# Other byte offsets for the weight blocks of the 256-column products in a two-layer encoder kernel

## The chip, the cores and the metric

The kernel runs on one core of a Trainium2 chip, in one launch. The metric is the device time of that launch in microseconds. Before the change three timed runs gave a median of 1366.84 us (1366.77 to 1368.76).

## What is computed

The reference is a trunk of two encoder layers on 512 tokens of width 1024, in float32. Each layer has a token mixer and a channel mixer, each between two RMS norms, with a residual sum:

```
hn = rms_norm(x, norm_mix_pre)
m  = retention_na_mixer(hn, ...)        # layer 0: retention beside 2-D neighbourhood attention
m  = ssd_mixer(hn, ...)                 # layer 1: bidirectional Mamba-2 mixer
x  = x + rms_norm(m, norm_mix_post)
u  = depthwise_conv_centered(rms_norm(x, norm_ffn_pre) @ w_up, conv_w, conv_b)   # 1024 -> 2 x 2816
gate, val = split(u, 2)
f  = (gelu(gate) * val) @ w_down        # 2816 -> 1024
x  = x + rms_norm(f, norm_ffn_post)
```

Most of the time is matrix products with weights from DRAM: the input projections of the mixers, and `w_up` and `w_down` of the channel mixers.

## The kernel before, in words

**Products in three terms.** TensorE takes float32 operands here in a one-pass format (float32r). To keep the precision, each operand is split into a high part and a low part: ScalarE casts the source to the high part and VectorE subtracts it from the source for the low part (`split`, lines 115 and 116). A product is then three matmuls that add up in one PSUM bank (`mm3`, lines 124 to 126): high weights with high data (L124), low weights with high data (L125), high weights with low data (L126). Each matmul first loads 128 x 128 weights into the array (LDWEIGHTS, the engine PEld of the profile), then streams 512 or 256 columns of data. One 128 x 128 block of weights is 128 float32 wide, 512 bytes in each partition.

**The ring.** A weight unit of 128 x 1024 float32 lands from DRAM in a staging tile `wst` and is split into a place of `ring`. The ring has four places, taken in turn (`weight`, line 82). A place is 2,048 + 128 float32 wide, 8,704 bytes or 17 x 512, and the ring begins on a multiple of 512 bytes; so all four places lie alike within 512 bytes. The 128 spare floats (`GAP`) let the two parts be shifted:

```
SKEW, GAP = 16, 128                      # line 29
a, b = skew, 1024 + GAP - 3 * skew       # in weight(): starts of the high and the low part
```

With `skew=0` both parts begin on a 512-byte boundary (0, and 1,152 floats or 9 x 512 bytes). With `skew=SKEW` of 16 the high part begins 64 bytes behind a boundary and the low part at 1,104 floats, 4,416 bytes, which is 320 behind one. Since all eight blocks of a part follow at 512 bytes, every weight load from that part has the same offset. The data operands (`xh`, `xl` and the combinations below) begin on multiples of 512 bytes in every product.

**Where 256 columns are streamed.** Nearly all products stream 512 columns and use `skew=0`. Three places stream 256 columns and use `skew=SKEW`:

- *Strassen blocks.* Of the 22 column groups of 128 in each half of `w_up` (gate and value), four pairs (`UP`, line 396: 6, 10, 14, 18) are computed by Strassen's scheme with seven products where there would be eight (`up_strassen`, line 437). A product is 2 x 4 x 3 = 24 matmuls of 256 columns. Its weights are made by `weights(i)` (line 458), which loads, adds and splits into the ring through `parts` (line 450). Its data are `A11`, `A12`, `A22` (parts of `xh`, `xl`) or the combinations `R1`, `S3`, `S2`, `S4` (`combos`, line 399), in the fixed order of line 480. With four blocks in each of two layers that makes 8 blocks, 56 products and 1,344 matmuls.
- *The start of each feed-forward stage* (`ffn`, from line 531). Four units, two column groups of gate and value each, run first over tokens 0 to 255 and then over tokens 256 to 511, since the last two token tiles are still being normalised and transposed when the first half begins (`E.flush()`, line 546, issues those transposes between the units). Two units lie in the ring, the third in two tiles `b1h` and `b1l` (high and low apart), the fourth in one tile `s3` (both parts). `extra` (line 526) places these at `SKEW` floats behind the tile's start, so both parts have 64 bytes. 4 x 2 x 8 x 3 = 192 matmuls in each layer. In the second layer the first two units are made ahead, in `trunk` (line 1334).
- *The start of mixer 1* (line 1228). Three units in the ring, in the same two halves: 144 matmuls.

The order of the work is written out by hand in the source, with priorities for the splits. One queue (SP's) issues the weight loads, POOL's issues the DRAM-to-DRAM sums of `w_down`.

Of the kernel before, what the change touches and what calls it, by code (L numbers as in the profile page):

```python
# [25 lines left out]
HK = NF // 2  # L26
HW = S // 2
QUARTER = HK * P * S
SKEW, GAP = 16, 128


class Env:
# [49 lines left out]
    def weight(self, skew=0):  # L82

        place = self.ring[:, self.turns % 4]
        self.turns += 1
        a, b = skew, 1024 + GAP - 3 * skew
        return place[:, a:a + 1024], place[:, b:b + 1024]

    def wunit(self, src, parts=None, st=None, behind=None, low_behind=None, skew=0):
# [347 lines left out]
def up_strassen(E, w_up, f, X, G, V):  # L437

    nc, tc = E.nc, E.tc
    low, high = slice(0, HW), slice(HW, S)

    def load(pool, name, s, h):
        st = pool.tile([P, 1024], F32, name=name)
        nc.sync.dma_start(st.rearrange("p (f c) -> p f c", f=2),
                          w_up[s, f:f + 2, :, h * 512:h * 512 + 512].rearrange("f p c -> p f c"))
        return st

    def parts(st):  # L450
        hi, lo = E.weight(SKEW)
        E.split(hi, lo, st)
        return hi, lo

    add = lambda o, x, y: nc.vector.tensor_tensor(o, x, y, op=ALU.add)
    q = {}

    def weights(i):
        with tc.high_priority(60):
            if i == 0:  # L460
                q[11] = load(E.wst, "wst", 0, 0)
                return parts(q[11])
            if i == 1:
                q[12], q[22] = load(E.wst, "wst", 1, 0), load(E.wst, "wst", 1, 1)
                add(q[11], q[11], q[12])
                add(q[12], q[12], q[22])
                return parts(q[12])
            if i == 2:
                q[0] = E.gain.tile([P, D], F32, name="gain")
                add(q[0], q[11], q[22])  # L470
                return parts(q[0])
            if i == 3:
                q[21] = load(E.gain, "gain", 0, 1)
                add(q[0], q[0], q[21])
                return parts(q[0])
            return parts(q[{4: 11, 5: 21, 6: 22}[i]])

    a = [E.mm.tile([P, S], F32, name="mm") for _ in range(2)]
    b, d = ([E.px.tile([P, S], F32, name="pu", tag="px") for _ in range(2)] for _ in range(2))
    order = ("A11", a), ("S3", b), ("S2", a), ("A22", b), ("R1", a), ("A12", d), ("S4", a)  # L480
    for i, (n, bank) in enumerate(order):
        hi, lo = weights(i)
        more = i in (2, 3, 4, 6)
        for j in range(2):
            for k in range(4):
                c = slice(j * 512 + k * P, j * 512 + k * P + P)
                E.mm3(bank[j][:, :HW], hi[:, c], lo[:, c], X[n][0][:, k], X[n][1][:, k], not more and k == 0, k == 3, more)
        if i == 4:
            t = E.tmp.tile([P, 2, HW], F32, name="w5", tag="tmp")
        for j in range(2):  # L490
            r = bank[j][:, :HW]
            if i in (3, 5):
                o = G[:, j, low if i == 3 else high]
                add(o, r, o)
            else:
                o = t[:, j] if i == 4 else {0: G[:, j, high], 1: V[:, j, low], 2: G[:, j, low], 6: V[:, j, high]}[i]
                nc.scalar.copy(o, r)
        if i == 4:
            add(V[:, :, low], t, V[:, :, low])
        if i in (2, 5):  # L500
            E.chore(2)


def ffn(E, w_up, cw, w_down, ts, g_post_row, done, w1=None):


    nc, tc = E.nc, E.tc
    with ExitStack() as ctx:
        hp, cp = (ctx.enter_context(tc.tile_pool(name=n, bufs=1)) for n in ("ffn_h", "ffn_c"))
        H = hp.tile([P, NF, S], F32, name="H")  # L510

        def conv(ps, s, f, neg=False):
            w = lambda i: (cwn[:, f] if neg and i < 3 else cwt[:, s, f])[:, i:i + 1]
            o = E.tmp.tile([P, S], F32, name=f"cv{s}", tag="tmp")
            nc.scalar.activation(o, ps, AF.Identity, scale=w(1), bias=w(3))  # L515
            nc.vector.scalar_tensor_tensor(o[:, 1:], ps[:, :S - 1], w(0), o[:, 1:], op0=ALU.mult, op1=ALU.add)  # L516
            nc.vector.scalar_tensor_tensor(o[:, :S - 1], ps[:, 1:], w(2), o[:, :S - 1], op0=ALU.mult, op1=ALU.add)  # L517
            return o

        def tail(f, pg, pv, neg=False):  # L520
            g = conv(pg, 0, f)
            nc.scalar.activation(g, g, AF.Gelu_apprx_tanh)  # L522
            v = conv(pv, 1, f, neg)
            nc.vector.tensor_tensor(H[:, f], g, v, op=ALU.mult)

        def extra(tags):
            t = [hp.tile([P, SKEW + 2048 // len(tags)], R32, name="x" + n, tag=n)[:, SKEW:] for n in tags]
            t = t if len(t) == 2 else [t[0][:, :1024], t[0][:, 1024:]]
            return [x[:, c:c + 512] for x in t for c in (0, 512)]

        u0, u1, st = w1 or (E.wunit(w_up[0, 0], skew=SKEW), E.wunit(w_up[1, 0], skew=SKEW), None)

        behind = E.turned[1][1] if w1 else None
        w0 = [[u0, u1], [E.wunit(w_up[0, 1], extra(("b1h", "b1l")), st, behind=behind),
                         E.wunit(w_up[1, 1], extra(("s3",)), behind=behind)]]
        cwt = cp.tile([P, 2, NF, 4], F32, name="cwt")
        nc.sync.dma_start(cwt, cw)
        cwn = cp.tile([P, NF, 3], F32, name="cwn")
        nc.vector.tensor_scalar(cwn, cwt[:, 1, :, :3], -1.0, None, op0=ALU.mult)
        p0 = [[E.mm.tile([P, S], F32, name="mm") for s in range(2)] for f in range(2)]  # L540
        for c in range(2):
            for i in range(4):
                f, s = i // 2, i % 2
                E.proj_fm(p0[f][s], w0[f][s], c * 256, c * 256 + 256)
                if c == 0 and i in (1, 2):
                    E.flush()
        for f in range(2):
            tail(f, *p0[f])
        make = combos(E, hp, H[:, 14:].rearrange("p (n g) s -> p n (g s)", n=4).rearrange("p n (k c) -> p n k c", k=4))
        for f in range(2, NF):  # L550
            if f in UP or f - 1 in UP:
                if f in UP:
                    G, V = (cp.tile([P, 2, S], F32, name=n, tag=t) for n, t in
                            ((("G", "k0"), ("V", "k1")) if UP.index(f) % 2 else (("G", "k2"), ("V", "k3"))))
                    up_strassen(E, w_up, f, X, G, V)
                    for j in range(2):
                        tail(f + j, G[:, j], V[:, j], True)
                continue
            ps = []
            for s in range(2):  # L560
                behind = w1 and f == 2
                st = E.wload(w_up[s, f], E.mid if behind and s == 0 else None)
                w = E.wunit(None, st=st, behind=E.turned[3][1] if behind else None)
                ps.append(E.mm.tile([P, S], F32, name="mm"))
                E.proj_fm(ps[-1], w)
            tail(f, *ps)
            E.chore(2)
            if f < UP[0]:
                X = next(make)
            if f == NF - 2:  # L570
                first = [hp.tile([P, HK, HW], R32, name="a" + n, tag=n) for n in ("b1h", "b1l")]
                for k in range(0, HK, 4):
                    c = slice(k, min(k + 4, HK))
                    E.split(first[0][:, c], first[1][:, c], H[:, c, HW:])
        g_post = E.bcast(g_post_row)
        down_strassen(E, hp, cp, w_down, ts, H, first, g_post, done)
# [331 lines left out]
def mixer1(E, w_dt, w_fm, cw, dtc, cols, mask, w_out, g_post_row, done, ahead):  # L908
# [8 lines left out]
    with ExitStack() as ctx:  # L917
# [307 lines left out]
                project(o, i)  # L1225
            silus(o)

        w0 = [E.wunit(w_fm[0, i], skew=SKEW) for i in range(3)]
        p0 = [E.mm.tile([P, S], F32, name="mm") for _ in range(3)]
        for c in range(2):  # L1230
            for i, (w, ps) in enumerate(zip(w0, p0)):
# [11 lines left out]
        for g, o in enumerate(gs):  # L1243
            nx = gs[g + 1] if g + 1 < NG else None
            for step in SLOTS[g].split():
                a, i = step[0], int(step[1:] or 0)
# [22 lines left out]
        st = {}  # L1269
# [19 lines left out]
def trunk(tc, x, norms, ab, ssd, ffns, out):  # L1289

    nc = tc.nc
    with ExitStack() as ctx:
        E = Env(ctx, tc)
        w0 = []
# [35 lines left out]
        w1 = []  # L1330

        def ahead(w):
            up = ffns[1][0]
            w1.extend((E.wunit(up[0, 0], skew=SKEW), E.wunit(up[1, 0], low_behind=w, skew=SKEW), E.wload(up[0, 1])))

        mixer1(E, *ssd, norms[1, 1], then(norms[1, 2]), ahead)
        E.chores = sums(E, ffns[1][2], ts[1])
        ffn(E, *ffns[1], ts[1], norms[1, 3], store, w1)
        while E.late:
            E.flush()  # L1340
# [119 lines left out]
```

## Time and profile before

| What | Value |
|---|---|
| median of the three timed runs | 1366.84 us |
| device time of the profiled execution | 1368.77 us |
| its span, first to last instruction | 1367.0 us |
| mean granted TensorE clock | 0.999 |
| LDWEIGHTS busy | 1133.3 us |
| matmuls with `ring` weights over `xh`, `xl`, 512 columns | 840 each of L124, L125, L126, mean 392 ns |
| the same with 256 columns | 176 each, mean 281 ns |
| Strassen block in the span | 343.0 to 362.8 us (first), 1213.7 to 1233.4 us (last) |

A row of the timeline gives the start from the span's beginning, the duration, the engine, the line, and output <- inputs by the program's names with buffer numbers left out. All products of `mm3` carry the lines 124 to 126, so they are told apart by the tiles: `pu<-xh,ring` is a Strassen product with a bank of the pool `px`, `mm<-xS,ring` one with a combination S as data. `mm<-xh,xs` is the fourth unit of a feed-forward start. Durations of matmuls overlap, since one starts before the one ahead of it has drained; the rate is read from start to start.

### The profile page before, as it was taken

Reading aid. Unit: us, or ns where it says so; the run is one execution under the profiler, and the core shown is the slowest. Engines: PE = TensorE matmul, PEld = TensorE weight load, DVE = VectorE, ACT = ScalarE, POOL = GpSimd, SP = SyncE. Lnnn points to the kernel's source line nnn. Section 1 sums busy time; section 2 is a strip of 40 time slices with the busy share of each in tenths; the row PEclk is TensorE's granted clock in tenths of the full one; section 3 lists DMA queues with packets and bytes.
Section 4 is the critical chain, followed back from the end, with each engine's and each line's share of the span. In section 5 each row is a group of like instructions: output and inputs, shape, how many; then the busy total and the mean of one; then the engine's idle time right before and its main releaser. Section 6 shows DMA issues by size and latency. Waiting matters only on the chain.

```text
span 1367.0 us, 19496 instructions
## 1 busy us (share of the span) xinstructions
PE 1341.5 (98%) x7352; PEld 1133.3 (83%) x7352; DVE 1087.6 (80%) x1524; ACT 813.5 (60%) x1345; POOL 112.6 (8%) x130
## 2 busy tenths in 40 slices
PE   7999999999999999999999999999999999999997
PEld 6877777898999888888778788777878899998886
DVE  7468888697768889697878876898789887788876
ACT  5356667453554566664878787477555455556563
POOL 1011110100111100020000110000010001110000
PEclk9999999999999999999999999999999999999999
DMA  7443223126779945654566465174434678994554
GB/s 294 138 148 91 99 89 105 46 97 219 253 208 234 252 152 190 198 204 130 138 185 194 121 188 165 53 200 112 146 129 131 225 248 215 231 252 127 198 179 145
DMA packets 73471, 229.90 MB, mean 168 GB/s; under 512 B 8352, under 2 KB 9120, under 8 KB 72864
## 3 DMA queue, kind: packets, MB, share of 16 engines
q1 hardware_dynamic: 58320, 167.30, 37.5%
q0 software_dynamic: 7168, 46.14, 13.5%
q10 hardware_dynamic: 7888, 15.21, 4.2%
q8 instruction: 58, 0.95, 0.3%
q14 instruction: 37, 0.30, 0.1%
HBM read 221.01 MB, written 51.64 MB: 199 GB/s over the span
## 4 chain that ended last, share of the span: by engine, by line
PE 83%; DVE 6%; ACT 4%; DMA 3%; issue 2%; POOL 1%; SPq 0%; DVEq 0%; POOLq 0%; ACTq 0%
PE mm L124 23%; PE mm L126 23%; PE mm L125 23%; DMA pb<-pd 2%; PE pu L126 2%; PE pu L125 2%; PE pu L124 2%; PE pi L1126 1%; PE st L1075 1%; DVE ring L116 1%; PE py L1146 1%; DMA wst<-in_c_fm 1%; ACT pb L1105 1%; PE pt L181 1%; PE y L805 1%
## 5 line engine op out<-in xcount | busy, mean ns | idle before, releaser
L124 PE MATMUL mm<-xh,ring 128*128 128x512 f32 (+1 forms) x1024 | 382.0, 373 | 0.9 <-ACT z L1045 0.5
L126 PE MATMUL mm<-xl,ring 128*128 128x512 f32 (+1 forms) x1024 | 381.1, 373 | 1.0 <-DVE xl L116 0.5
L125 PE MATMUL mm<-xh,ring 128*128 128x512 f32 (+1 forms) x1024 | 380.8, 372 | 1.0 <-DVE ring L116 1.0
L116 DVE TENSOR_TENSOR ring<-wst,ring 128x1024 fp32r<-128x1024 f32 (+1 forms) x232 | 279.9, 1211 | 90.0 <-ACT ring L115 89.3
L115 ACT CAST ring<-wst 128x1024 fp32r<-128x1024 f32 (+1 forms) x232 | 239.0, 1034 | 150.1 <-PE mm L125 73.2
L124 PEld LDWEIGHTS mm<-xh,ring 128*128 128x128 f32 x1024 | 191.9, 187 | 36.3 <-issue 2.3
L126 PEld LDWEIGHTS mm<-xl,ring 128*128 128x128 f32 x1024 | 191.6, 187 | 35.5 <-issue 1.3
L125 PEld LDWEIGHTS mm<-xh,ring 128*128 128x128 f32 x1024 | 192.3, 188 | 34.3 <-DVE ring L116 1.4
L1105 ACT ACTIVATE pb<-pb,tok 128x128 f32<-128x128 f32 x256 | 80.8, 393 | 7.2 <-DMA pb<-pd 6.1
L515 ACT ACTIVATE cv<-mm,cwt 128x512 f32<-128x512 f32 x56 | 43.3, 776 | 62.9 <-PE mm L126 62.7
L124 PE MATMUL mm<-ring,ab1h 128*128 128x512 f32 x164 | 64.0, 390 | 0.0
L126 PE MATMUL mm<-ring,ab1h 128*128 128x512 f32 x164 | 63.9, 390 | 0.0
L125 PE MATMUL mm<-ring,ab1l 128*128 128x512 f32 x164 | 63.8, 389 | 0.0
L516 DVE SCALAR_TENSOR_TENSOR cv<-mm,cwt,cv 128x511 f32<-128x511 f32 x56 | 41.7, 745 | 21.2 <-ACT cv L515 21.2
L522 ACT ACTIVATE cv<-cv 128x512 f32<-128x512 f32 x44 | 27.8, 631 | 44.7 <-DVE cv L517 44.7
L1039 DVE SCALAR_TENSOR_TENSOR xf<-mm,cwt,xf 128x511 f32<-128x511 f32 (+1 forms) x64 | 47.5, 744 | 7.7 <-ACT xf L1036 7.3
L282 POOL DMA_DIRECT2D ts<-in_f_down x48 | 30.0, 658 | 259.6 <-PE mm L126 225.6
L517 DVE SCALAR_TENSOR_TENSOR cv<-mm,cwt,cv 128x511 f32<-128x511 f32 x56 | 41.7, 746 | 0.9
L1158 POOL TENSOR_TENSOR sq<-sq 128x512 f32<-128x512 f32 x11 | 16.7, 1514 | 309.2 <-ACT sq L1152 246.0
L124 PE MATMUL mm<-ring,yh 128*128 128x512 f32 x104 | 40.8, 394 | 0.7 <-DVE xf L1039 0.7
L124 PE MATMUL mm<-ring,xh 128*128 128x512 f32 x104 | 41.3, 404 | 0.0
L125 PE MATMUL mm<-ring,yl 128*128 128x512 f32 x104 | 41.1, 395 | 0.0
(359 smaller groups left out, 2918.1 us busy)
## 6 DMA issues: line engine op xcount, KB each, us to landing
wst<-in_f_up SPq DMA_DIRECT2D x80, 512.0 KB
ts<-in_f_down POOLq DMA_DIRECT2D x48, 704.0 KB, 6.1
wst<-in_c_fm SPq DMA_DIRECT2D x40, 512.0 KB
wst<-ts SPq DMA_DIRECT2D x32, 512.0 KB
pb<-pd ACTq DMA_DIRECT2D x29, 512.0 KB
wst<-in_f_down SPq DMA_DIRECT2D x24, 512.0 KB
ts<-ts POOLq DMA_DIRECT2D x16, 704.0 KB, 9.7
wst<-in_ab_fm SPq DMA_DIRECT2D x20, 512.0 KB
```

What stands on the lines that cost most here:

```text
L115: first = self.nc.scalar.copy(hi, src)
L116: second = self.nc.vector.tensor_tensor(lo, src, hi.bitcast(F32), op=ALU.subtract)
L124: mm(out, lh, rh, start=first, stop=False)
L125: mm(out, ll, rh, start=False, stop=False)
L126: self.product = mm(out, lh, rl, start=False, stop=last)
L282: out.append(lambda i=i, src=src, j=j, c=c, kw=kw: gp.dma_start(part(ts, i, c), part(src, j, c), **kw))
L515: nc.scalar.activation(o, ps, AF.Identity, scale=w(1), bias=w(3))
L516: nc.vector.scalar_tensor_tensor(o[:, 1:], ps[:, :S - 1], w(0), o[:, 1:], op0=ALU.mult, op1=ALU.add)
L517: nc.vector.scalar_tensor_tensor(o[:, :S - 1], ps[:, 1:], w(2), o[:, :S - 1], op0=ALU.mult, op1=ALU.add)
L522: nc.scalar.activation(g, g, AF.Gelu_apprx_tanh)
L1039: nc.vector.scalar_tensor_tensor(r[:, a], ps[:, b], wc(j), r[:, a], op0=ALU.mult, op1=ALU.add)
L1105: nc.scalar.activation(pb[:, dr, c], pb[:, dr, c], AF.Identity, scale=1.0 - 2 * dr, bias=tok[:, 0, c, dr * H + h:dr * H + h + 1])
```

## The change

`SKEW` becomes 48, and the low part begins at `1024 + GAP - skew // 3`. So a skewed ring place has its high part at 192 bytes within 512 and its low part at 1,136 floats, 4,544 bytes, which is 448 within 512. The distance of the two is 256 bytes within 512, as before. The tiles of `extra` have both parts at 192 bytes.

The first product of each Strassen block (`i == 0`) no longer uses the skew: its two parts begin on the boundary. The same holds for the first unit of each feed-forward start and of mixer 1's start. No instruction is added, removed or moved on any engine: the rows of all five engines are the same in the two programs, and only start addresses differ.

```diff
-SKEW, GAP = 16, 128
+SKEW, GAP = 48, 128
...
-        a, b = skew, 1024 + GAP - 3 * skew
+        a, b = skew, 1024 + GAP - skew // 3
...
-    def parts(st):
-        hi, lo = E.weight(SKEW)
+    def parts(st, i):
+        hi, lo = E.weight(SKEW if i else 0)
...
-                return parts(q[11])
+                return parts(q[11], i)
...
-        u0, u1, st = w1 or (E.wunit(w_up[0, 0], skew=SKEW), E.wunit(w_up[1, 0], skew=SKEW), None)
+        u0, u1, st = w1 or (E.wunit(w_up[0, 0]), E.wunit(w_up[1, 0], skew=SKEW), None)
...
-        w0 = [E.wunit(w_fm[0, i], skew=SKEW) for i in range(3)]
+        w0 = [E.wunit(w_fm[0, i], skew=SKEW if i else 0) for i in range(3)]
...
-            w1.extend((E.wunit(up[0, 0], skew=SKEW), E.wunit(up[1, 0], low_behind=w, skew=SKEW), E.wload(up[0, 1])))
+            w1.extend((E.wunit(up[0, 0]), E.wunit(up[1, 0], low_behind=w, skew=SKEW), E.wload(up[0, 1])))
```

More of the change, by code (lines that the diff above doesn't have):

```diff
@@ L466, in weights @@
                 add(q[12], q[12], q[22])
-                return parts(q[12])
+                return parts(q[12], i)
             if i == 2:
@@ L470, in weights @@
                 add(q[0], q[11], q[22])
-                return parts(q[0])
+                return parts(q[0], i)
             if i == 3:
@@ L474, in weights @@
                 add(q[0], q[0], q[21])
-                return parts(q[0])
-            return parts(q[{4: 11, 5: 21, 6: 22}[i]])
+                return parts(q[0], i)
+            return parts(q[{4: 11, 5: 21, 6: 22}[i]], i)
     a = [E.mm.tile([P, S], F32, name="mm") for _ in range(2)]
```

## The prediction

> **What bounds the kernel now.** I read the page first: busy time by engine, the clock in slices, the chain of waits.
>
> ```profile
> span 1367.0 us, 19496 instructions
> PE 1341.5 (98%) x7352; PEld 1133.3 (83%) x7352; DVE 1087.6 (80%) x1524; ACT 813.5 (60%) x1345; POOL 112.6 (8%) x130
> PEclk9999999999999999999999999999999999999999
> PE 83%; DVE 6%; ACT 4%; DMA 3%; issue 2%; POOL 1%; SPq 0%; DVEq 0%; POOLq 0%; ACTq 0%
> ```
>
> TensorE is busy for 98% of the span at full granted clock, and 83% of the chain that ended last is its own matmuls. Next, the waits of TensorE (total us, times, longest):
>
> ```profile
> PE pt L181 <- DVE xs L172: 9.7, 4, 7.3
> PE mm L124 <- ACT xh L115: 1.2, 2, 1.0
> ```
>
> The largest is the very start of the kernel (a norm before the first transposes), and the next is 1.2 us. So nothing is to be won from waits. A change of addresses alone can only move the time if it changes how fast matmuls follow each other, or how long VectorE and ScalarE take to write the operands. So the view that matters is the timeline of TensorE inside a Strassen block (columns: start in us, duration in us, line, operation). This is the first of the eight blocks, its first and its last rows:
>
> ```profile
> 342.77 0.39 PE L126 MATMUL mm<-xl,ring 128*128 128x512 f32 x1
> 343.00 0.28 PE L124 MATMUL mm<-xh,ring 128*128 128x256 f32 x1
> 343.12 0.28 PE L125 MATMUL mm<-xh,ring 128*128 128x256 f32 x1
> 343.24 0.28 PE L126 MATMUL mm<-xl,ring 128*128 128x256 f32 x1
> ...
> 362.67 0.28 PE L126 MATMUL mm<-xS,ring 128*128 128x256 f32 x1
> 362.79 0.40 PE L124 MATMUL mm<-xh,ring 128*128 128x512 f32 x1
> ```
>
> From 343.00 to 362.79 the block's 7 x 24 = 168 matmuls start one after another: 19.79 us / 168 = 117.8 ns from start to start, with no idle time. The durations (0.28 us) overlap and say nothing about the rate; the step between starts does. Now the start of the second feed-forward stage, where the same kind of product, from the same ring, at the same 64 and 320 bytes, runs behind a wait for VectorE:
>
> ```profile
> 1020.10 0.39 PE L126 MATMUL mm<-xl,ring 128*128 128x256 f32 x1 [0.51 <-DVE xl L116]
> 1020.32 0.28 PE L124 MATMUL mm<-xh,ring 128*128 128x256 f32 x1
> 1020.44 0.28 PE L125 MATMUL mm<-xh,ring 128*128 128x256 f32 x1
> 1020.56 0.28 PE L126 MATMUL mm<-xl,ring 128*128 128x256 f32 x1
> 1020.68 0.28 PE L124 MATMUL mm<-xh,ring 128*128 128x256 f32 x1
> 1020.79 0.28 PE L125 MATMUL mm<-xh,ring 128*128 128x256 f32 x1
> ...
> 1022.49 0.28 PE L125 MATMUL mm<-xh,ring 128*128 128x256 f32 x1
> ```
>
> From 1020.79 to 1022.49 there are 15 steps: 1.70 / 15 = 113.3 ns. So these products have two regular steps, a long one of 117.8 ns and a short one of 113.3 ns. The minimum, median and maximum of durations show how regular each is. In the Strassen blocks, and then in the stretch from 1020.4 to 1022.2:
>
> ```profile
> L124 PEld LDWEIGHTS pu<-xh,ring x128: 187/188/188, 351.4 to 1230.1; 128*128 128x128 f32 x128
> L125 PEld LDWEIGHTS pu<-xh,ring x128: 192/192/192, 351.5 to 1230.3; 128*128 128x128 f32 x128
> L125 PE MATMUL pu<-xh,ring x128: 281/281/281, 351.6 to 1230.4; 128*128 128x256 f32 x128
> ```
>
> ```profile
> L125 PE MATMUL mm<-xh,ring x6: 276/276/283, 1020.4 to 1022.2; 128*128 128x256 f32 x6
> ```
>
> In the long step every matmul takes 281 ns without exception and every third weight load 192 instead of 188; in the short step matmuls take 276. Both hold themselves: each goes on until something disturbs it. And offset alone does not choose between them. The fourth unit of each feed-forward start has both its parts at 64 bytes; it runs long in the first layer and short in the second:
>
> ```profile
> 285.44 0.28 PE L125 MATMUL mm<-xh,xs 128*128 128x256 f32 x1
> ...
> 287.91 0.28 PE L125 MATMUL mm<-xh,xs 128*128 128x256 f32 x1
> ```
>
> ```profile
> 1030.09 0.28 PE L126 MATMUL mm<-xl,xs 128*128 128x256 f32 x1
> ...
> 1030.77 0.28 PE L126 MATMUL mm<-xl,xs 128*128 128x256 f32 x1
> ```
>
> That is 2.47 / 21 = 117.6 ns, and 0.68 / 6 = 113.3 ns. What chooses is how the stretch is entered: from a stream of 512-column products (all eight Strassen blocks) it becomes the long step; behind a late operand, as at 1020.10, it passes a few uneven steps and becomes the short one.
>
> **The change, part by part.** No engine's instructions are moved, added or removed; only start addresses differ. So the sum has no term for instructions or queues.
>
> The first product of each Strassen block now lies on the boundary. The nearest rows are mixer 0's score products, also 256 columns with the weights on a 512-byte boundary, in short runs:
>
> ```profile
> 140.58 0.28 PE L789 MATMUL sc<-rql,rk 128*128 128x256 f32 x1
> ...
> 141.29 0.28 PE L789 MATMUL sc<-rql,rk 128*128 128x256 f32 x1
> ```
>
> ```profile
> 173.15 0.28 PE L789 MATMUL sc<-rql,rk 128*128 128x256 f32 x1
> ...
> 173.87 0.28 PE L789 MATMUL sc<-rql,rk 128*128 128x256 f32 x1
> ```
>
> ```profile
> L789 PE MATMUL sc<-rql,rk x32: 278/282/283, 89.4 to 219.2; 128*128 128x256 f32 x32
> ```
>
> Six steps take 0.71 and 0.72 us, 118.3 and 120.0 ns (starts are printed to 10 ns, so 1.7 ns either way), mean 119.2. And they are uneven: durations run from 278 to 283, where a settled stretch has one value. So 8 x 24 = 192 matmuls cost 119.2 - 117.8 = 1.4 ns more each: +0.3 us; bounds -0.9 us (113.3 ns) and +0.4 us (120.0).
>
> The other six products of each block move from 64/320 to 192/448 bytes and are entered from that uneven run and no longer from the 512-column stream: 8 x 6 x 24 = 1,152 matmuls. No row shows 192 or 448 bytes. The bounds are the two settled steps and the slowest boundary run: 113.3 (-5.2 us), 117.8 (0), 120.0 (+2.5 us). I take 113.3, because the one thing that precedes the short step in this trace is a handful of uneven steps, and the boundary product supplies 24 of them; because the short step exists at two different offset pairs (64/320 and 64/64), so it isn't bound to one; and because everything between 113.3 and 117.8 would have to be a third regular step that no row shows.
>
> The three stage starts (two feed-forward, one mixer 1) have 192 + 192 + 144 matmuls of 256 columns, a first unit on the boundary and the rest at the new offsets. Their first halves are cut by transposes or waits, so I leave them as they are. In the second half of each feed-forward start, long today in the first layer and over most of the second, three units of 24 follow the boundary unit: 2 x 72 x 4.5 ns = -0.65 us. Mixer 1's second half is short today, and its boundary unit loses 24 x 5.9 = +0.14 us. Sum -0.5 us, bounds -1.5 (all of the starts short) and +0.7 (mixer 1's 96 and the second layer's 40 short ones lost, at up to 5.9 ns).
>
> Writing the parts: ScalarE and VectorE write the same shapes to other offsets; bounds zero either way, since both engines have slack in the blocks. The cover is thinnest in the last block:
>
> ```profile
> 1213.70:1233.50 19.80, 19.80 (x170) 19.80 (x169) 18.06 (x20) 13.73 (x22) 1.75 (x2) 1.00 0.87 234
> ```
>
> VectorE (fourth figure after the colon, 18.06 of 19.80 us) still has 1.74 us; a block shorter by 6 x 24 x 4.5 = 0.65 us leaves 1.09. If that cover were gone, up to 2 x 0.65 us (the last block of each feed-forward) would come back as waits.
>
> Sum: -5.2 + 0.3 - 0.5 = -5.4 us. The profiled execution took 1368.77 us (span 1367.0 and 1.8 around it), so it would become 1363.4. It lies 1.9 us above the median of the three timed runs, 1366.84; against that median the forecast is 1361.4.
>
> The Trainium skill speaks on the size of the short step. In "TensorE: Matmul & The Clock Gate", section "Back-to-back issue gap", the isolated gap at full clock is columns / 2.4 + 2.5 ns, by which an estimate for 256 columns is 109.2 ns, and the 1,152 matmuls would gain 9.9 us. The shortest settled step measured here is 113.3, and the sum goes by that.
>
> **The rivals.** 0.2% is 2.7 us, about what a measurement of this kernel can tell from no change.
>
> *The long step stays (same).* The offset changes nothing and the entry leads back into the long step: 0 for the 1,152, between 0 and +0.4 for the boundary products, +-0.7 for the starts: 1366.1 to 1367.9. For it: the long step survives changes of unit and of offset (it runs from ring to 64/64 units and back in the first layer), and eight entries of eight in Strassen blocks lead to it. Against it: the entry is what the change alters, and boundary runs aren't settled. The same result would follow if two operands of TensorE never met in SBUF. The skill says so ("TensorE: Matmul & The Clock Gate", section "Step-by-step: what each phase is for"): the moving operand and the weight load have separate read ports, so loading the next weights takes nothing from the running matmul. Two step lengths for one kind of product, with 188 and 192 ns loads, speak against taking that as the whole story, but they do not show the address to matter.
>
> *Some blocks only.* The order in which the uneven run ends decides anew at each block or product. With half of the products short the gain is 2.7 us: 1364.1, at the edge of faster.
>
> *The new offsets stay uneven (slower).* At 192/448 nothing locks, and all products run like the boundary run. At 120.0 ns, (1,152 + 192) x 2.2 = +3.0 us in the blocks and up to +0.7 in the starts: 1370.5. It is slower by over 0.2% only from a mean step of 117.8 + 2.7 us / 1,344 = 119.8 ns on; the score runs with a mean of 119.2 lie just below.
>
> **How the numbers follow.** Short step in the blocks: 0.48. Some of them: 0.08, split evenly over the bound. Long step, or a step within 2 ns of it: 0.33. Uneven at 119.8 ns or more: 0.11. So faster 0.52, same 0.37, slower 0.11. The predicted time is the first case's, 1361.4. Its own range is 1360.1 (all starts short as well, and first products no slower than the long step: -5.2 - 1.5) to 1363 (a product more per block lost on the way to the short step, 8 x 24 x 4.5 = 0.9 us, and the starts' +0.7). The range of 8 in 10 must take in the second case too, up to 1368.0, and leaves out the slower one.
>
> **What would show it.** In the timeline of the changed kernel the first block starts its second product about 2.86 us after its first; then steps of 113.3 ns and durations of 276 show the first case, 117.8 and 281 with 192-ns loads the second, spread durations the last. A whole block should take 24 x 119.2 + 144 x 113.3 = 19.2 us, where it takes 19.8 now. The forecast is wrong if the block stays at 19.8, or if it shrinks and the following 512-column products wait for VectorE.

## The result and the profile after

The changed kernel takes 1362.78 us, the median of six runs (1361.55 to 1364.75); six runs of the kernel before, beside it, have a median of 1367.88. The ratio is 0.9964 with an interval of 0.9953 to 0.9975. In a second comparison it was 0.9972 (0.9963 to 0.9982; medians 1363.87 and 1367.87). Both ratios are more than 0.2% below 1; the first interval is so as a whole, the second reaches up to 0.18%. Both intervals hold -4.8 us (a ratio of 0.9965), which the trace accounts for below.

The page of the changed kernel, the same two lines as before:

```profile
span 1361.1 us, 19496 instructions
PE 1335.2 (98%) x7352; PEld 1127.2 (83%) x7352; DVE 1087.1 (80%) x1524; ACT 813.3 (60%) x1345; POOL 111.1 (8%) x130
```

Nothing moved between engines, and VectorE and ScalarE are as busy as they were. TensorE's busy time fell by 6.3 us and its weight loads' by 6.1. The waits of TensorE that lead its list (total us, times, longest):

```profile
PE pt L181 <- DVE xs L172: 9.6, 4, 7.3
PE mm L124 <- DVE xf L1039: 1.5, 2, 1.3
PE mm L125 <- DVE ring L116: 1.5, 1, 1.5
```

The first is the norm at the start, as before. The other two stood in the kernel before as well, at the same places and with 0.9 and 1.0 us; in the profile of the second comparison they have 0.9 and 1.0 again, so the 1.1 us more in this execution is not the change's. So the gain must lie in the step. The timeline of TensorE in the first Strassen block, at its entry, at the change from the first product to the second, and at its end:

```profile
340.89 0.39 PE L126 MATMUL mm<-xl,ring 128*128 128x512 f32 x1
341.12 0.28 PE L124 MATMUL mm<-xh,ring 128*128 128x256 f32 x1
...
344.00 0.28 PE L124 MATMUL pu<-xS,ring 128*128 128x256 f32 x1
...
360.20 0.28 PE L126 MATMUL mm<-xS,ring 128*128 128x256 f32 x1
360.31 0.40 PE L124 MATMUL mm<-xh,ring 128*128 128x512 f32 x1
```

The first product takes 2.88 us / 24 = 120.0 ns a step, the other six 16.31 / 144 = 113.3 ns. The whole block takes 19.19 us where it took 19.79. All eight blocks do the same, to 0.01 us: 8 x 0.60 = -4.8 us. (Rows are printed to 10 ns, and a product's time includes the step on which it is entered, so over 24 matmuls a mean is good to some 0.4 ns; inside the boundary product the step is 120.0.) How regular they are is seen in minimum, median and maximum of the durations, in the six products behind the first one:

```profile
L124 PEld LDWEIGHTS pu<-xh,ring x128: 187/188/188, 349.3 to 1224.4; 128*128 128x128 f32 x128
L125 PEld LDWEIGHTS pu<-xh,ring x128: 187/188/188, 349.4 to 1224.5; 128*128 128x128 f32 x128
L125 PE MATMUL pu<-xh,ring x128: 276/276/276, 349.5 to 1224.6; 128*128 128x256 f32 x128
```

The weight loads of L125 took 192 ns before, and all take 188 now; every matmul takes 276 where every one took 281. In the boundary product itself all eight loads of L125 are long (the group in the stretch from 341.2 to 343.9: busy us, mean ns), and the matmuls of L124 last 283 ns:

```profile
L125 PEld LDWEIGHTS mm<-xh,ring 128*128 128x128 f32 x8 | 1.5, 192 | 0.0
```

```profile
L124 PE MATMUL mm<-xh,ring x8: 278/283/283, 341.1 to 343.6; 128*128 128x256 f32 x8
```

The boundary product is even, then, in the blocks: a third regular step. The cover in the last block held:

```profile
1208.40:1227.60 19.20, 19.20 (x170) 19.20 (x169) 18.08 (x20) 13.60 (x22) 1.75 (x2) 1.00 0.90 241
```

VectorE is busy for 18.08 of 19.20 us, 1.12 us of slack where 1.09 was forecast, and TensorE fills the stretch.

The three stage starts did not gain. The second half of the first layer's start, by the first rows of its boundary unit and of the next unit, and the first 512-column product behind it:

```profile
286.23 0.28 PE L124 MATMUL mm<-xh,ring 128*128 128x256 f32 x1
...
289.11 0.28 PE L124 MATMUL mm<-xh,ring 128*128 128x256 f32 x1
...
297.59 0.40 PE L124 MATMUL mm<-xh,ring 128*128 128x512 f32 x1
```

The boundary unit takes 2.88 / 24 = 120.0 ns, but the three units behind it 8.48 / 72 = 117.8, the long step. Here the boundary unit is not even: the loads of L125 have a mean of 189 instead of 192, and the matmuls run from 280 to 287, in a pattern of five steps (117, 118, 121, 120 and 124 ns) that repeats to the unit's end and has the same mean of 120.0.

```profile
L125 PEld LDWEIGHTS mm<-xh,ring 128*128 128x128 f32 x8 | 1.5, 189 | 0.0
```

```profile
L124 PE MATMUL mm<-xh,ring x8: 280/283/287, 286.2 to 288.8; 128*128 128x256 f32 x8
```

In mixer 1's second half it is otherwise: the boundary unit, whose start is broken up by a wait, is settled from 626.0 us on, with 120 ns from start to start and loads of 192 (the group in the stretch from 625.6 to 626.6), and the 113.3 that this half had before follows it.

```profile
L125 PEld LDWEIGHTS mm<-xh,ring 128*128 128x128 f32 x4 | 0.8, 192 | 0.0
```

In the second layer's start the second half is long in this execution. In the profiled execution of the same kernel in the second comparison, it is short:

```profile
1039.04 0.28 PE L124 MATMUL mm<-xh,xs 128*128 128x256 f32 x1
...
1041.87 0.40 PE L124 MATMUL mm<-xh,ring 128*128 128x512 f32 x1
```

```profile
1039.06 0.28 PE L124 MATMUL mm<-xh,xs 128*128 128x256 f32 x1
...
1041.78 0.40 PE L124 MATMUL mm<-xh,ring 128*128 128x512 f32 x1
```

The last unit takes 2.83 / 24 = 117.9 ns in the one and 2.72 / 24 = 113.3 in the other. So one program goes either way there, behind waits whose length differs from execution to execution. The first halves, which the prediction left as they were, did change: in the first layer the first unit lost 0.05 us at the boundary and the second, now at 113.3 up to the transposes, gained 0.10. From the first 256-column product to the first 512-column product behind it the three starts take 24.37, 19.83 and 26.54 us before, 24.37, 19.97 and 26.59 after, and 24.37, 19.95 and 26.28 in the second comparison: together 0.2 us more and 0.1 us less than before.

The two profiled spans differ by 5.9 us, more than the blocks' 4.8. Of this, 1.9 us arises ahead of the first 256-column product with ring weights (at 275.1 us of the span before, 273.2 after), where the change has touched nothing. From there to the end the difference is 1091.9 - 1087.9 = 4.0 us: the blocks' 4.8 less 0.8, for which the two longer waits of 1.1 us are enough. Single runs of one kernel lie up to 4 us apart, so these remainders aren't followed further.

### The profile page after: what moved, and what is told of

Its sections match the earlier page's. It is cut to its first block, busy times and chain, and to the rows that moved or that the text cites. A ratio compares the mean times of both kernels' runs of the same rounds, so it can differ in the third digit from the quotient of the medians.

```text
span 1361.1 us, 19496 instructions
## 1 busy us (share of the span) xinstructions
PE 1335.2 (98%) x7352; PEld 1127.2 (83%) x7352; DVE 1087.1 (80%) x1524; ACT 813.3 (60%) x1345; POOL 111.1 (8%) x130
## 4 chain that ended last, share of the span: by engine, by line
PE 85%; DVE 5%; ACT 4%; DMA 2%; issue 2%; POOL 1%; DVEq 0%; SPq 0%; POOLq 0%; ACTq 0%
PE mm L124 23%; PE mm L126 23%; PE mm L125 23%; PE pu L126 2%; PE pu L124 2%; PE pu L125 2%; PE st L1075 2%; PE pi L1126 1%; PE py L1146 1%; DMA wst<-in_c_fm 1%; DVE ring L116 1%; ACT ring L115 1%; PE pt L1019 1%; PE pt L181 1%; PE y L805 1%
## 5 line engine op out<-in xcount | busy, mean ns | idle before, releaser
L124 PE MATMUL mm<-xh,ring 128*128 128x512 f32 (+1 forms) x1024 | 382.1, 373 | 0.4 <-ACT xh L115 0.2
L125 PE MATMUL mm<-xh,ring 128*128 128x512 f32 (+1 forms) x1024 | 381.0, 372 | 1.5 <-DVE ring L116 1.5
L124 PEld LDWEIGHTS mm<-xh,ring 128*128 128x128 f32 x1024 | 192.2, 188 | 35.4 <-issue 2.5
L125 PEld LDWEIGHTS mm<-xh,ring 128*128 128x128 f32 x1024 | 192.2, 188 | 34.8 <-DVE ring L116 1.9
L124 PE MATMUL mm<-ring,ab1h 128*128 128x512 f32 x164 | 64.0, 390 | 0.0
L125 PE MATMUL mm<-ring,ab1l 128*128 128x512 f32 x164 | 63.8, 389 | 0.0
L124 PE MATMUL mm<-ring,yh 128*128 128x512 f32 x104 | 40.8, 394 | 1.3 <-DVE xf L1039 1.3
L125 PE MATMUL mm<-ring,yl 128*128 128x512 f32 x104 | 41.1, 395 | 0.0
L124 PE MATMUL mm<-ring,xh 128*128 128x512 f32 x104 | 40.7, 398 | 0.0
```

What stands on the lines that cost most here:

```text
L124: mm(out, lh, rh, start=first, stop=False)
L125: mm(out, ll, rh, start=False, stop=False)
```

## The experiments

Each of the kernels below computes the whole reference. "Pair a/b" are the offsets of the high and the low part within 512 bytes. A block step is the mean from start to start in the blocks of one profiled execution. A product's step includes the one on which it is entered, so a boundary product that runs at 120.0 inside reads 119.5 to 120.0. In the sweeps a count of the blocks, `block`, picks the pair, and only the Strassen blocks differ from the changed kernel unless it is said. Line numbers stay, except in the first two sweeps, where they are one higher.

**One half of the change each.** Either the boundary product alone leads to the short step, whatever the offsets behind it, or the new offsets alone do. The first kernel keeps the boundary product and puts the other products back to 64/320:

```diff
-SKEW, GAP = 48, 128
+SKEW, GAP = 16, 128
...
-        a, b = skew, 1024 + GAP - skew // 3
+        a, b = skew, 1024 + GAP - 3 * skew
```

> The first product of each Strassen block on the boundary, as in the changed kernel, and the others back at 64 and 320 bytes. Entry theory (the uneven or settled boundary product decides how the rest is entered, and any offset off the boundary holds the short step): the first product at 120.0 ns a step, the other six at 113.3, a block of 19.2 us, time as the changed kernel, 1362.8 us. Offset theory (192 and 448 bytes hold the short step, 64 and 320 do not): after the boundary product 117.8 ns, a block of 19.85 us, time 1368.3 us, 0.4 us above before.

The second takes the kernel before and only moves the skewed parts to 192/448, the same two lines the other way round:

> All products of 256 columns at 192 and 448 bytes, none on the boundary. Entry theory: the entry from 512-column products leads to the long step as before, 117.8 ns throughout, a block of 19.8 us, time 1367.9 us. Offset theory: 113.3 ns throughout, a block of 19.04 us, time 1361.5 us.

The first took 1369.11 us beside 1367.71 of the kernel before, ratio 1.0008 (1.0000 to 1.0017). The second took 1367.98, ratio 1.0002 (0.9993 to 1.0011). The timelines of the first block, boundary product alone and then new offsets alone:

```profile
341.60 0.28 PE L124 MATMUL mm<-xh,ring 128*128 128x256 f32 x1
...
344.47 0.28 PE L124 MATMUL pu<-xS,ring 128*128 128x256 f32 x1
...
361.43 0.40 PE L124 MATMUL mm<-xh,ring 128*128 128x512 f32 x1
```

```profile
341.40 0.28 PE L124 MATMUL mm<-xh,ring 128*128 128x256 f32 x1
...
361.19 0.40 PE L124 MATMUL mm<-xh,ring 128*128 128x512 f32 x1
```

With the boundary product alone: 2.87 / 24 = 119.6, then 16.96 / 144 = 117.8. With the offsets alone: 19.79 / 168 = 117.8 throughout. Neither half does anything by itself, and both theories fall: the gain belongs to the two together. At 64/320 the boundary product was even, at 120.0 inside, and the long step followed all the same.

**All eight pairs, without and with a boundary product.** Each of the eight blocks gets its own pair, so one execution shows eight. Since all eight blocks behave alike wherever they share a pair (the kernel before, the changed kernel, the two above), a difference between blocks is put down to the pair. `OFFS` lists the pairs:

```diff
-        hi, lo = E.weight(SKEW if i else 0)
+        hi, lo = E.weight(OFFS[block])
```

> The eight Strassen blocks at eight pairs of offsets in turn (16/272, 32/288, 64/320, 96/352, 128/384, 160/416, 192/448, 224/480 bytes), no product on the boundary. Entry theory: 117.8 ns in all eight blocks. Offset theory: 117.8 in the third, 113.3 in the seventh, and others that show where the border lies.

```diff
-        hi, lo = E.weight(SKEW if i else 0)
+        hi, lo = E.weight(OFFS[block] if i else 0)
```

> The same eight pairs, each block behind a first product on the boundary. Entry theory: 120.0 ns in the first product and 113.3 in the other six of all eight blocks. Offset theory: 113.3 in the seventh block and 117.8 in the third, with the others as in the sweep without a boundary product.

The times of one execution each, 1368.71 and 1369.48 us, are sums over eight cases. The steps are what was wanted, in ns, over all starts of the block and over those behind the boundary product; the boundary product's own step is 119.6 to 119.7 in every block, 120.0 inside it:

| Pair of the block | all seven products | the six behind a boundary product |
|---|---|---|
| 16/272 | 118.3 | 118.3 |
| 32/288 | 118.3 | 118.3 |
| 64/320 | 117.8 | 117.8 |
| 96/352 | 117.3 | 117.3 |
| 128/384 | 120.0 | 118.6 |
| 160/416 | 119.9 | 119.9 |
| 192/448 | 117.8 | **113.3** |
| 224/480 | 116.7 | 116.7 |

The offsets alone do set a step, between 116.7 and 120.0 ns, and the pairs of the kernel before and of the changed one give the same 117.8. Behind a boundary product 192/448 falls by 4.5 ns and 128/384 by 1.4; the other six stay. (The expectations of later runs quote 118.6, 118.4 and 120.2 from this sweep, where whole blocks give 118.3, 118.3 and 119.9.)

**Is 192/448 able, or is it led?** If the short step only has to be reached, any pair should keep it that is entered in it. The boundary product is followed by two at 192/448, and the last four of each block take its own pair (`offs` gives the boundary for product 0, 192/448 for 1 and 2, and the pair of the block from there on):

```diff
-        hi, lo = E.weight(SKEW if i else 0)
+        hi, lo = E.weight(offs(block, i))
```

> In each Strassen block the first product is on the boundary, the second and third at 192/448 bytes (113.3 ns in the changed kernel), and the last four at a pair that differs by block: 16/272, 32/288, 64/320, 96/352, 128/384, 160/416, 192/448, 224/480. Lock theory (the short step holds itself at any offset, only the way into it depends on the offset): 113.3 ns in products two to seven of all eight blocks. Offset theory (of these pairs 192/448 alone can hold the short step): the last four products take the step of the sweep without a boundary, 118.6, 118.4, 117.8, 117.3, 120.0, 120.2, 113.3 and 116.7 ns.

It took 1368.38 us in one execution (the kernel before 1371.51 on that chip). In the first block the last four are at 16/272, in the third at 64/320:

```profile
351.46 0.28 PE L124 MATMUL pu<-xh,ring 128*128 128x256 f32 x1
...
362.82 0.40 PE L124 MATMUL mm<-xh,ring 128*128 128x512 f32 x1
...
434.38 0.28 PE L124 MATMUL pu<-xh,ring 128*128 128x256 f32 x1
...
445.26 0.40 PE L124 MATMUL mm<-xh,ring 128*128 128x512 f32 x1
```

At 16/272 the four products take 11.36 / 96 = 118.3 ns; at 64/320 they take 10.88 / 96 = 113.3. The other pairs fall back to 118.3 (32/288), 117.3, 118.6, 119.9 and 116.6 (224/480). So two pairs of the eight can keep the short step, the old one among them. What 64/320 lacks in the first kernel above is the way into it.

**What leads 192/448 into it.** The first product takes eight other pairs, the rest of the block stays at 192/448 (`offs` gives the pair of the block for product 0 alone):

```diff
-        hi, lo = E.weight(SKEW if i else 0)
+        hi, lo = E.weight(offs(block, i))
```

> The first product of each block at a pair that differs by block (16/272, 32/288, 64/320, 96/352, 128/384, 160/416, 0/256, 224/480), the other six at 192/448. Boundary theory (only a first product on the boundary, with its 120.0 ns a step, leads to the short step): 117.8 ns in products two to seven of all eight blocks. Phase theory (any first product whose step differs from 117.8 ns hands over at another phase): 113.3 ns behind the pairs with another step, the fifth and sixth (120.0 and 120.2 ns) above all, and 117.8 behind 64/320.

It took 1366.44 us. Steps of the first product and of the rest: 16/272 118.3 and 117.8; 32/288 118.3 and 117.8; 64/320 117.9 and 117.8; 96/352 117.5 and 117.8; 128/384 120.3 and 117.8; 160/416 119.6 and 113.3; 0/256 119.7 and 113.3; 224/480 116.6 and 113.3. The rows for 128/384 and for 160/416:

```profile
1088.36 0.29 PE L124 MATMUL mm<-xh,ring 128*128 128x256 f32 x1
...
1091.24 0.28 PE L124 MATMUL pu<-xS,ring 128*128 128x256 f32 x1
...
1108.21 0.40 PE L124 MATMUL mm<-xh,ring 128*128 128x512 f32 x1
...
1130.04 0.28 PE L124 MATMUL mm<-xh,ring 128*128 128x256 f32 x1
...
1132.91 0.28 PE L124 MATMUL pu<-xS,ring 128*128 128x256 f32 x1
...
1149.23 0.40 PE L124 MATMUL mm<-xh,ring 128*128 128x512 f32 x1
```

Two first products of nearly the same step (2.88 and 2.87 us) lead to 16.97 / 144 = 117.8 and to 16.32 / 144 = 113.3. So it isn't the boundary as such, nor a slow step, nor merely another offset. Nor is it evenness: in the products at 160/416 and 224/480, which work, the matmuls last from 278 to 286 and from 278 to 282 ns. Three of the eight pairs tried lead into the short step; what they have in common isn't shown.

**Where the boundary product stands.** If what matters is the boundary product itself, it should work at any place in the block; if it has to meet the 512-column stream ahead of the block, only at the first. `PLACE` moves it to the first, second, and so on to the sixth product, and in two blocks there are two of them (`offs` gives the boundary where the product is in `PLACE` of the block, else 192/448):

```diff
-        hi, lo = E.weight(SKEW if i else 0)
+        hi, lo = E.weight(offs(block, i))
```

> All products at 192/448 bytes but the one on the boundary, whose place in the block differs: first, second, third, fourth, fifth, sixth, then first and fourth, then second and third. Reset theory (a boundary product, wherever it stands, leads whatever follows at 192/448 into the short step): 117.8 ns ahead of it, about 120 in it, 113.3 behind it. Entry theory (it must be entered from the 512-column stream): only the first and the seventh block have 113.3, and in the seventh the boundary product in fourth place ends it or not; the others stay at 117.8. The second halves of the feed-forward starts, which stayed long behind a boundary unit, speak for the second.

It took 1368.1 us. In the fourth block the boundary product is the fourth:

```profile
469.11 0.28 PE L124 MATMUL pu<-xS,ring 128*128 128x256 f32 x1
...
474.76 0.28 PE L124 MATMUL pu<-xh,ring 128*128 128x256 f32 x1
...
477.63 0.28 PE L124 MATMUL mm<-xR,ring 128*128 128x256 f32 x1
...
485.79 0.40 PE L124 MATMUL mm<-xh,ring 128*128 128x512 f32 x1
```

The second and third product take 5.65 / 48 = 117.7 ns, the boundary product 2.87 / 24 = 119.6, the three behind it 8.16 / 72 = 113.3. All eight blocks keep to this: the long step ahead of the first boundary product, the short one behind it, with blocks of 19.19 us (boundary at the first place), 19.29, 19.40, 19.51, 19.61 and 19.72 (at the sixth). With two boundary products in a block (first and fourth, 19.35; second and third, 19.45), each takes 119.5 to 120.0 and the products behind it 113.3. Inside a block the boundary product resets the step wherever it stands, and the entry from 512 columns plays no part.

**A faster first product.** 224/480 also leads into the short step and has a shorter step of its own. First products and first units take it:

```diff
-SKEW, GAP = 48, 128
+SKEW, GAP = 48, 128; FIRST = 56, 1024 + 120; offs = lambda g, i: SKEW if i else FIRST
...
-        hi, lo = E.weight(SKEW if i else 0)
+        hi, lo = E.weight(offs(block, i))
...
-        w0 = [E.wunit(w_fm[0, i], skew=SKEW if i else 0) for i in range(3)]
+        w0 = [E.wunit(w_fm[0, i], skew=SKEW if i else FIRST) for i in range(3)]
```

> As the changed kernel, but each first product (and first unit of the three stage starts) at 224/480 bytes in place of the boundary. In the run with eight different first products this pair stepped at 116.5 ns and was followed by 113.3. Expected: blocks of 24 x 116.5 + 144 x 113.3 = 19.12 us, 0.07 us less than the changed kernel's 19.19, 0.6 us in eight blocks; in the starts between 0 and -0.7 us more if the second halves become short as well. So 0.6 to 1.3 us below the changed kernel in the same comparison; if the starts stay long, their first units alone gain 6 x 24 x 3 ns = 0.4 us.

With it, on the same chip, ran the changed kernel once more:

> The changed kernel itself, on the same chip as the one with first products at 224/480, for a direct comparison: 0.9964 of before, about 5 us less.

They took 1363.63 us (ratio to before 0.9970, 0.9959 to 0.9981) and 1363.87 (0.9972, 0.9963 to 0.9982). The blocks are 0.07 us shorter, 19.12 with steps of 116.6 and then 113.3, together -0.6 us. Against that, mixer 1's second half went over to the long step (116.7 behind its wait, then 117.6 and 117.7), the first layer's start stayed long, and the second layer's was long in this execution. The medians differ by 0.2 us where 0.6 to 1.3 were expected, and the intervals overlap: the times can't tell the two kernels apart.

**Finer pairs and other distances.** Pairs between those of the first sweep, without a boundary product (`offs` gives the pair of the block for all seven):

```diff
-        hi, lo = E.weight(SKEW if i else 0)
+        hi, lo = E.weight(offs(block, i))
```

> No boundary product; eight more pairs with 256 bytes between the parts: 48/304, 80/336, 112/368, 176/432, 208/464, 216/472, 240/496 and 248/504 bytes. Smooth theory (the step is set by where in the stream of the data the load meets it): values between those of the coarse sweep, 48/304 near 118, 80/336 near 117.5, 112/368 between 117.3 and 120, 176/432 near 119, 208/464 near 117.2, 240/496 from 116 down to 113.3. Granule theory (only multiples of 32 or 64 bytes differ): each equals its neighbour. A pair at 113.3 from its first product on would need no first product of another kind.

It took 1368.8 us. 48/304 118.3; 80/336 118.6; 112/368 120.0; 176/432 118.1; 208/464 116.7; 216/472 119.9; 240/496 117.3; 248/504 117.6. From 208 to 216 bytes the step rises by 3.2 ns. It is neither smooth in the offset nor the same over granules of 32 or 64 bytes, and no pair reaches 113.3 from the 512-column stream.

The next one, with other distances between the two parts, gave no answer on them:

> No boundary product; the eight blocks with other distances of the two parts: 0/256, 0/384, 0/448, 192/192, 224/224, 192/256, 192/0 and 256/0 bytes. If the distance of 256 bytes matters little, the steps stay between 116.7 and 120.2 ns as in the sweep, and 192/192 is at 117.8. If what counts is the offset of each load by itself, pairs with one part on the boundary lie between 117.8 and 120.0 ns, two thirds of the way to the high part's value, since two of three loads are of the high part. A pair at 113.3 without a boundary product would be a better kernel by 8 x 24 x 6.7 = 1.3 us.

Its one execution took 3469.28 us, because all of TensorE's work, changed or not, was slower in it. The page, and the groups of a TensorE and a VectorE line (busy us, mean ns):

```profile
PE 3453.4 (100%) x7352; PEld 2298.3 (66%) x7352; DVE 1112.6 (32%) x1524; ACT 825.0 (24%) x1345; POOL 105.7 (3%) x130
```

```profile
L124 PE MATMUL mm<-xh,ring 128*128 128x512 f32 (+1 forms) x1024 | 799.8, 781 | 0.0
L116 DVE TENSOR_TENSOR ring<-wst,ring 128x1024 fp32r<-128x1024 f32 (+1 forms) x232 | 279.6, 1206 | 574.3 <-ACT ring L115 574.1
```

The matmul group has a mean of 781 ns where the changed kernel has 373; the VectorE group has 1206 where it has 1216. A lower clock of TensorE would fit, and nothing here rules it out: its page has no row of the granted clock, as every other page here has, and its trace holds no record of it. The eight blocks took 49.98 to 50.11 us, whatever their pair. Nothing on offsets at the usual speed follows. The same pairs ran again in the next kernel, in a normal execution.

**The starts.** In the changed kernel the fourth unit of a feed-forward start has both parts at one offset (192/192). If that is why the boundary unit doesn't lead to the short step there, 192/448 for the third and fourth unit should cure it. The same kernel gives each Strassen block a pair of another distance, without a boundary product:

```diff
-            t = [hp.tile([P, SKEW + 2048 // len(tags)], R32, name="x" + n, tag=n)[:, SKEW:] for n in tags]
-            t = t if len(t) == 2 else [t[0][:, :1024], t[0][:, 1024:]]
+            t = [hp.tile([P, 112 + 2048 // len(tags)], R32, name="x" + n, tag=n) for n in tags]
+            t = [t[0][:, 48:1072], t[1][:, 112:1136] if len(t) == 2 else t[0][:, 1136:2160]]
...
-        hi, lo = E.weight(SKEW if i else 0)
+        hi, lo = E.weight(offs(block, i))
```

> Two questions in one look. The starts: the third and fourth units of the feed-forward starts have their parts at 192 and 448 bytes, where the changed kernel has both at 192. In the changed kernel's first layer the second half runs long behind its boundary unit, which is entered from the fourth unit. If that unit's equal offsets hand over at the wrong phase, the boundary unit now settles at 120.0 ns with durations of 283, and the three units behind it step at 113.3; if the boundary unit leads to the short step only behind 512 columns or inside Strassen blocks, they stay at 117.8. The Strassen blocks, without a boundary product, have other distances of the two parts: 0/256, 0/384, 0/448, 192/192, 224/224, 192/256, 192/0 and 256/0 bytes. If each load counts by its own offset, the pairs with the high part on the boundary are near 120.0 ns and 192/192 is at 117.8; if the distance of 256 bytes matters, the other distances leave the range of 116.7 to 120.2.

It took 1367.53 us (the kernel before 1368.17). The first layer's second half, by the same three rows as above:

```profile
286.39 0.28 PE L124 MATMUL mm<-xh,ring 128*128 128x256 f32 x1
...
289.27 0.28 PE L124 MATMUL mm<-xh,ring 128*128 128x256 f32 x1
...
297.75 0.40 PE L124 MATMUL mm<-xh,ring 128*128 128x512 f32 x1
```

Again 2.88 us and then 8.48 / 72 = 117.8 ns. The equal offsets are not the cause. The pairs of other distances ran at 120.0 (0/256), 119.0 (0/384), 117.7 (0/448), 117.8 (192/192, 192/256 and 192/0), 116.7 (224/224) and 120.0 (256/0). None leaves the range of the first sweep. Nor does each load count by its own offset as was expected: with the high part on the boundary, 0/448 ran at 117.7, not near 120.

## Why the prediction came out as it did

**The place of the gain and the main term are right.** 1361.4 us was forecast and 1362.78 measured; 1.0 of the 1.4 us between them is the kernel before, whose median is 1367.88 over six runs and was 1366.84 over three. -5.4 us was forecast, and the change of the medians is -5.1 (by the ratio, -6.4 to -3.4); the blocks account for -4.8. The 1,152 matmuls went from 117.8 to 113.3 ns, -5.2 us as forecast, in every block alike; the rivals of the long step, of some blocks only and of uneven new offsets didn't come. No wait took the gain back.

**The boundary products were mis-sized, slightly.** 119.2 ns and +0.3 us were forecast; measured were 120.0 inside the product, 119.7 with its entry, and +0.4 (192 x 1.9 ns). That they would be uneven, as mixer 0's short runs are, was wrong in the blocks: there they settle, at 283 ns with loads of 192.

**The starts' term failed.** -0.5 us was forecast from units that go short behind a boundary unit. Six of the experiments above change the blocks alone, so with the two of the changed kernel eight profiles share these starts: the first layer's second half is long in all eight, the second layer's short in three. What differs is visible: where the boundary product becomes even (loads 192, matmuls 283), in the blocks, in mixer 1 and in those three, the short step follows; where it keeps to the pattern of five steps (loads 188 to 189, matmuls 280 to 287), the long one does. Equal offsets of the fourth unit were tried as the cause and are not. That the stream ahead decides which of the two it becomes remains a guess: ahead of the first layer's second half run 256-column products at the long step, yet in the blocks with a later boundary product (fourth block above) the same long step at 192/448 stands ahead, and there it becomes even. What sets this apart stays open. Two of the prediction's bounds around this term are also a little off: 136 matmuls x 5.9 ns are 0.8 us and not 0.7, and the first case's upper end, with that bound in place of the -0.5, is 1363.6 us and not 1363.

**The reason for 113.3 was only partly right.** Three statements carried it. That the entry decides was right: at 192/448 the same instructions run at 117.8 or 113.3 depending on the product ahead. That the boundary product works because it supplies uneven steps was wrong: in the blocks it is even and works, it doesn't work ahead of 64/320 (ratio 1.0008), and where it is uneven, in the starts, it fails; of the uneven first products at other pairs, those at 160/416 and 224/480 work and the one at 128/384 doesn't. And that a value between the two steps "would have to be a third regular step that no row shows" was no argument: the sweeps found some ten values from 116.7 to 120.0 ns, each held from product to product. Had the change chosen any other of the seven pairs, the same words would have forecast 113.3, and by the sweep behind a boundary product the blocks would have come out between 0.9 us faster (224/480, 19.68 us a block) and 2.8 us slower (160/416, 20.14). That the pair of this change is one that a boundary product leads into the short step was, for this reasoning, luck.

**The long-step rival** was right in its point that eight entries of eight led to the long step at 64/320: a boundary product there changes nothing. It was wrong that the offset changes nothing: behind the same boundary product 192/448 goes short and 64/320 doesn't, though either can keep the short step.

## What to carry to other kernels

When TensorE is busy for the whole of a stretch, read the step from start to start, not the durations, and compare it between stretches of the same instruction: two settled values mean that something other than the amount of work sets the rate. The start address of the weights within 256 bytes is worth a sweep in one execution with a setting for each block, and what runs just ahead belongs to the setting. Move such offsets together with their predecessor, since each half alone gained nothing here (ratios 1.0008 and 1.0002).

## What the runs showed of the hardware

*The step of a one-pass float32 matmul of 256 columns depends on where its weights start.* With the same data and instructions it was 116.7 to 120.0 ns by offset, and 113.3, the shortest in any block, in a state that two of the eight pairs 256 bytes apart can keep, 64/320 and 192/448. Equal offsets keep it too: the fourth units of the second layer's start ran at 113.3 at 64/64 (kernel before) and at 192/192 (second comparison). Parts that differ by 256 bytes gave the same step: 0/256 and 256/0 the 120.0 of the boundary, 192/192 the 117.8 of 192/448, 224/224 the 116.7 of 224/480, 192/0 the 117.8 of 192/256. So the pattern seems to repeat each 256 bytes. The Trainium skill ("TensorE: Matmul & The Clock Gate", section "Step-by-step: what each phase is for") says that the weight load has an SBUF port of its own and takes nothing from the running matmul, and "SBUF — State Buffer", section "Who interferes with whom", that TensorE never waits on anyone. The runs here differ from a reading of these by which addresses can't matter: a spread of 6.7 ns, 6%, with nothing changed but the weights' place. They don't show where in the machine it arises, in the reading of the weights, of the data, or in how loads and matmuls take turns.

*A settled state outlives what caused it.* In the changed kernel the short step lasts through the 144 matmuls behind the boundary product, over several data operands. A product at 16/272 behind it ended it, one at 64/320 didn't.

*One execution of 3469 us had all of TensorE's work stretched*, the group of L124 from a mean of 373 to 781 ns, with VectorE unchanged. Its profile has no record of the granted clock, so whether the clock was lower stays open.
